# Moving the making of the up projection's first operands, pinning the down projection's splits, and loading w_up's pass from another queue

## The chip, the core and the metric

The kernel runs on one core of a Trainium2 chip. The metric is the device time of one execution in microseconds. A core has TensorE (PE; its weight loads are listed as PEld), VectorE (DVE), ScalarE (ACT), GpSimd (POOL) and SyncE (SP), which here only issues DMAs. Each engine works through its own instructions in order.

## The reference

It is one decoder layer over 2048 rows of width 1024, in float32. `h2` below goes through an FFN of width 2816 with a causal convolution of three taps over the rows.

```python
h = rmsnorm(x, norm1_g) * (1 + sc1) + sh1
proj = h @ w_in                                   # q, k, v, forget logits, x_in, B, C
attn = forgetting_attention(q, k, v, logf)        # 8 heads of 64
conv = bg * causal_dwconv(cg * xin, conv_mix_w)
x = x + g1 * (concatenate([attn, conv]) @ w_out)
h2 = rmsnorm(x, norm2_g) * (1 + sc2) + sh2
u = causal_dwconv(h2 @ w_up, ffn_conv_w)
u_gate, u_val = split(u, 2)
return x + g2 * ((silu(u_gate) * u_val) @ w_down)
```

## The kernel before

To keep float32 accuracy, every matrix product is made from operands that are split in two: a rounded part `hi` and the rest `lo = raw - hi`. `mm3` (line 138) then issues three matmuls, hi·hi, hi·lo and lo·hi. A split costs one ACT operation for `hi` (L720) and one DVE operation for `lo` (L721).

The stages follow each other in the program:

- **Projections and short convolution** (to about 635 us). `project` makes k and then q in blocks of 128 rows. Beside them, `magnitudes` (lines 585 to 596) goes over the whole of w_up once, 88 tiles of 256 KB, and sums absolute values on ACT (L590), for a scale. It has one buffer `wx`: a load (L595, on SP) is issued after the sum before it.
- **Attention** (about 635 to 966 us). Steps s = 0 to 63, eight for each head. POOL writes the tile `wide`, a transposing DMA on SP (L892) turns it into `far`. `load_out` (line 728) loads one of 16 tiles of w_out on SP, and the function that it returns multiplies it with the gate g1 on POOL (L733).
- **Output projection** `mixed(Q)` for four quarters of 512 rows, in two halves of columns, each over eight k: 16 steps n. A step splits a tile of w_out and a tile of the mixed input. `side` is another generator, of which one part is run at the steps listed in `at`.
- **`norm2(Q)`** makes the operands of the up projection for a quarter: `columns` transposes on PE (L1047) and applies scale and shift on ACT (L1049), `operand` makes a float16 pair (ACT L1037, DVE L1038). The product h2 @ w_up is made for two quarters at once with seven block products in place of eight (a Strassen-like scheme), so the operands are sums and differences named b11, b21, b22, t1 to t4. For Q = 1, b22 and t4 are left to `norm2_rest` (lines 1101 to 1105), which calls `columns` once more.
- **`up(hv)`** for the halves hv = 0, 1 of the rows: 22 iterations, one for each 128 columns of the gate and the value. An iteration has seven products of 12 matmuls (L1167). `up_weights(i)` (line 1122) is a generator that loads two tiles of w_up, scales them (ACT L1132), and makes their sums and float16 pairs (DVE L1107, L1108, L1114; ACT L1111). It runs one iteration ahead. `finish(i)` (taps L1180, silu, product L1192, store to `y_sc`) runs one iteration behind.
- **`down(Q, hf)`**, four calls after each `up`: 22 pairs of tiles of y and w_down, loaded together into one raw tile (L1262, L1263), split, and multiplied.

The order in which a queue gets its instructions is made by a scheduler from the program's order and a model of the durations. `K(...)` pins an instruction: pinned instructions of an engine keep the program's order among themselves. All of `up` is pinned. The splits of `mixed` and `down` are not.

Tiles with one tag share a fixed number of buffers: `raw` 4, `hi` and `lo` 4 each, `t2` (`temp()`) 7.

Of the kernel before, what the change touches and what calls it, by code (L numbers as in the profile page):

```python
# [1 line left out]

# [6 lines left out]
F32 = mybir.dt.float32  # L9
# [35 lines left out]
def kernel(  # L45
# [102 lines left out]
    with ExitStack() as ph:  # L148
# [437 lines left out]
        def magnitudes():  # L586

            while up_tiles:
                n, t = up_tiles.pop(0)
                K(A.activation(t, t, AF.Abs, accum_out=l1[:, n : n + 1]))  # L590
                seen[0] = n + 1
            for n in range(seen[0], min(seen[0] + 1, 88)):
                t = bp.tile([P, 512], F32, tag="wx", name="wx", bufs=1)
                k, i = divmod(n, 11)
                K(nc.sync.dma_start(t, w_up[k * P : (k + 1) * P, i * 512 : (i + 1) * 512]))  # L595
                up_tiles.append((n, t))

        def up_scales():
# [151 lines left out]
    def mixed(Q, side=iter(()), at=()):  # L750

        rows = [slice((Q * 4 + t) * P, (Q * 4 + t + 1) * P) for t in range(4)]
        n = 0
        if Q:
            places(Q)
        if Q == 0:
            kept[0] = [raw_tile() for _ in range(4)]
        elif Q == 1:
            kept[1] = [wide_temp()[:, 0:D] for _ in range(4)]
        for hf in range(2):  # L760
            n0 = hf * 512
            acc = [ps_d.tile([P, 512], F32, tag="d", name="acc") for _ in range(4)]
            ops = []
            for k in order:
                if hf == 0 and (Q or k == 3):
                    load_mixed(Q, k)
                (mh, ml), (wh, wl) = halves(pair_tiles())
                split(wo[k, hf], wh, wl)
                split(src[Q, k], mh, ml)
                ops.append((mh, ml, wh, wl))  # L770
                for t in () if k == 2 else range(4):
                    for o in ops:
                        a, b = [m[:, t * P : (t + 1) * P] for m in o[:2]]
# [4 lines left out]
                if n in at:  # L778
                    next(side, None)
                if Q < 2 and n == (2, 4)[Q]:  # L780
                    for xp, r in zip(kept[Q], rows):
                        K(nc.sync.dma_start(xp, x[r, :]))
                if Q >= 2 and k == 0:
                    kept[Q] = [temp() for _ in range(4)]
                    for xp, r in zip(kept[Q], rows):
                        K(nc.sync.dma_start(xp, x[r, n0 : n0 + 512]))
                yield
            for t in range(4):
                xp = kept[Q][t]
                if Q < 2:  # L790
                    xp = xp[:, n0 : n0 + 512]
                V.tensor_tensor(xp, acc[t], xp, op=ALU.add)
                if Q >= 2:
                    G.dma_start(x1_sc[Q * 4 + t][:, n0 : n0 + 512], xp)
                elif hf:
                    G.dma_start(x1_sc[Q * 4 + t], kept[Q][t])


    with ExitStack() as ph:
# [159 lines left out]
        for s in range(H * nu + 8):  # L959
            h, u = divmod(s, nu)  # L960
            run = []
            if h < H:
                if u == 0:
                    steps = []
                    if h + 1 < H:
                        heads[h + 1], steps = load_head(h + 1)
                    if h % 2 == 0:
                        if h:
                            v16.append(load_values(h // 2))
                        at = cp.tile([P, NT, P], F32, tag="at", name="at")  # L970
                elif h + 1 < H:
                    steps[u - 1]()
                units.append({"h": h, "u": u, "at": at})
            for back, stage in ((1, weights), (0, scores), (2, turn), (4, values)):
                if 0 <= s - back < H * nu:
                    run.append(stage(units[s - back]))
            if s >= 16 and s % 16 in (0, 4):
                slow.append(store(units[s - 5]["at"], (s - 16) // 16, (0, 3) if s % 16 == 0 else (1, 2)))
            if s >= (H - 4) * nu and s % 2 == 0 and s < H * nu:
                gated = load_out((s - (H - 4) * nu) // 2)  # L980
            if s == (H - 1) * nu:
                places(0)
# [12 lines left out]
            if (H - 4) * nu <= s < H * nu and s % 2:  # L995
                gated()
            if s == H * nu:
                first = mixed(0)
            if s >= H * nu:
                next(first)  # L1000
# [11 lines left out]
    with ExitStack() as ph:  # L1012
# [47 lines left out]
        def norm2(Q):  # L1060
# [18 lines left out]
            for k in range(4):  # L1079
# [5 lines left out]
                b1 = columns(Q, k)  # L1085
                yield
                b2, t3 = columns(Q, 4 + k), temp()
                if Q == 3:
                    operand("b22", k, b2)
                diff(t3, b2, b1)  # L1090
                for e in bt["b11", k]:
                    diff(b1, b1, e)
# [1 line left out]
                diff(b2, b2, b1)  # L1094
                operand("t2", k, b2)
                operand("t3", k, t3)
                if Q == 3:
                    last_operands(Q, k)
                yield

        def norm2_rest(Q):
            for k in range(4):
                operand("b22", k, columns(Q, 4 + k))
                last_operands(Q, k)
                yield

# [10 lines left out]

        def up_pair():
            used[0] += 1
            return [fb.tile([P, 1024], F16, tag=f"wo{used[0] % 8}{e}", name="pair") for e in range(2)]  # L1120

        def up_weights(i):

            raws = raw_tile(), raw_tile()
            for raw, ct in zip(raws, (i, NPAIR + i)):
                nc.sync.dma_start(
                    raw.rearrange("p (k n) -> p k n", n=P), w_up[:, ct * P : (ct + 1) * P].rearrange("(k p) n -> p k n", p=P)
# [25 lines left out]
            low(raws[1], *pc)  # L1153
            yield

        def up(hv, side):


            def product(acc, pair, name, first):
# [33 lines left out]
                nc.sync.dma_start(y_sc[i][:, hv * 1024 : (hv + 1) * 1024], yv)  # L1193
                yield

            wts = up_weights(0)
            ops = next(wts)
            for _ in range(5):
                next(wts)
            last = None  # L1200
            for i in range(NPAIR):
                o11, o12, os2, os4, os3, o22, os1 = ops
# [9 lines left out]
                next(side, None)  # L1212
# [3 lines left out]
                K(A.activation(p1, X, AF.Copy))  # L1216
# [6 lines left out]
                next(side, None)  # L1223
# [6 lines left out]
                next(side, None)  # L1230
# [4 lines left out]
                next(side, None)  # L1235
                p5 = temp()
                K(A.activation(p5, Z, AF.Copy))
                product(Y, os3, "t3", False)
# [11 lines left out]
            for _ in last:  # L1250
                pass

        def down(Q, hf):
            n0 = hf * 512
            acc = [ps_d.tile([P, 512], F32, tag="d", name="acc") for _ in range(4)]
            w = [None] * NPAIR
            order = [(i, t) for i in range(NPAIR - 2) for t in range(4)]
            order += [(i, t) for t in range(4) for i in range(NPAIR - 2, NPAIR)]
            for i, t in order:
                if w[i] is None:  # L1260
                    raw = raw_tile()
                    nc.sync.dma_start(raw[:, 0:512], y_sc[i][:, Q * 512 : (Q + 1) * 512])  # L1262
                    nc.sync.dma_start(raw[:, 512:1024], w_down[i * P : (i + 1) * P, n0 : n0 + 512])  # L1263
# [12 lines left out]
            pass  # L1276
        for _ in mixed(1, norm2(0), (1, *range(5, 13))):
            pass
        steps = norm2(1)
        for _ in mixed(2, steps, (1, 5, 7, 10, 11, 14, 15)):  # L1280
            pass
        for _ in mixed(3, steps, (2, 3)):
            pass
        for hv in range(2):
            up(hv, iter(()) if hv else norm2_rest(1))
            for n in range(4):
                down(2 * hv + n // 2, n % 2)
                if hv == 0 and n < 2:
                    for _ in norm2(2 + n):
                        pass  # L1290
# [28 lines left out]
```

## Time and profile before

| what | value |
|---|---|
| three runs, median | 2508.15 us (2499.21 to 2508.64) |
| the profiled execution | 2507.0 us |
| its span, first to last instruction of the program | 2505.3 us |
| mean granted clock of TensorE | 0.989 |
| `up(0)`, first to last product | 1169.3 to 1596.2 us |
| four calls of `down` | 1596.2 to 1848.7 us |
| `up(1)` | 1848.5 to 2259.0 us |
| four calls of `down` | 2259.1 to 2500.8 us |

In a line of instructions the columns are line, engine, operation, names of what is written and read, shapes and count; then busy time and mean duration in ns; then the idle time of the engine ahead of them and who ended it. A line of waits has who waited, for whom, the sum in us, how often, and the longest. A line of windows has the window, its length, and for each engine the busy time and the count of instructions, then the granted clock of TensorE, the mean busy share of the DMA engines, and GB/s.

### The profile page before, as it was taken

The page shows a single profiled execution, that of the slowest core. Times are in us where ns is not written, and L with a number is a line of the kernel's source. Part 1 is how long each engine was busy: PE and PEld are TensorE (multiplying, and loading weights), DVE is VectorE, ACT ScalarE, POOL GpSimd, SP SyncE. Part 2 cuts the span into 40 slices and gives each one's busy share as a digit, 9 for nine tenths or more (in the row PEclk, how much of TensorE's full clock was granted, in tenths as well). Part 3 has the DMA queues.
Part 4 walks back from the last instruction along what each step waited for, and adds up shares of the span by engine and source line. Part 5 has one row for each costly group of instructions (what it writes and reads, how often), then busy time and mean ns, then how long its engine had stood idle before and what let it go on. Part 6 is the DMA issues. An engine that isn't in the chain of part 4 may idle for free. (4 is left out here: it accounts for less than half of the span.)

```text
span 2505.3 us, 38577 instructions
## 1 busy us (share of the span) xinstructions
PE 2388.9 (95%) x14432; PEld 1655.5 (66%) x14432; DVE 1814.0 (72%) x3377; ACT 1292.5 (52%) x2068; POOL 375.4 (15%) x314
## 2 busy tenths in 40 slices
PE   4999999999899889998999999999999999999999
PEld 4988778888677667776444444678764444447887
DVE  7567784342899887676888988667859888885554
ACT  3533443210788776554656566355545555553333
POOL 4210001011577873110000000000000000000000
PEclk9999999999999999999999999999999999999999
DMA  8444786433789997143222222567742222235775
GB/s 237 148 123 127 196 238 182 147 112 89 149 173 184 189 183 196 72 140 123 67 85 85 92 85 93 191 214 235 219 142 92 84 93 84 85 122 168 230 228 186
DMA packets 429348, 368.71 MB, mean 147 GB/s; under 512 B 184336, under 2 KB 328040, under 8 KB 428136
## 3 DMA queue, kind: packets, MB, share of 16 engines
q1 hardware_dynamic: 421976, 349.40, 50.0%
q10 hardware_dynamic: 4752, 8.46, 0.9%
q0 software_dynamic: 2432, 8.39, 0.9%
q8 instruction: 113, 1.85, 0.3%
q14 instruction: 75, 0.61, 0.1%
HBM read 267.54 MB, written 65.08 MB: 133 GB/s over the span
## 5 line engine op out<-in xcount | busy, mean ns | idle before, releaser
L1167 PEld LDWEIGHTS <-pair 128*128 128x128 f16 x3696 | 364.5, 99 | 470.2 <-issue 36.4
L1167 PE MATMUL acc<-t,pair 128*128 128x512 f16 x2112 | 482.5, 382 | 6.5 <-DVE t L1107 6.5
L1167 PE MATMUL acc<-b,pair 128*128 128x512 f16 x1584 | 372.5, 386 | 17.2 <-DVE pair L1114 6.6
L141 PE MATMUL acc<-hi 128*128 128x512 f32 x960 | 378.5, 395 | 7.9 <-ACT hi L720 5.7
L141 PE MATMUL acc<-hi,lo 128*128 128x512 f32 x960 | 375.8, 391 | 0.2 <-DVE lo L721 0.2
L141 PE MATMUL acc<-lo,hi 128*128 128x512 f32 x960 | 375.1, 391 | 0.0
L721 DVE TENSOR_TENSOR lo<-raw,hi 128x1024 fp32r<-128x1024 f32 (+1 forms) x208 | 236.3, 1142 | 178.8 <-ACT hi L720 178.6
L720 ACT ACTIVATE hi<-raw 128x1024 fp32r<-128x1024 f32 (+1 forms) x208 | 204.9, 991 | 240.4 <-PE acc L141 207.7
L1180 DVE SCALAR_TENSOR_TENSOR w<-w,fcw,w 128x1024 f32<-128x1024 f32 x176 | 226.1, 1285 | 39.9 <-ACT w L1175 30.8
L141 PEld LDWEIGHTS acc<-hi 128*128 128x128 f32 x960 | 180.7, 188 | 48.2 <-ACT hi L720 6.8
L141 PEld LDWEIGHTS acc<-hi,lo 128*128 128x128 f32 x960 | 180.6, 188 | 39.7 <-DVE lo L721 1.5
L141 PEld LDWEIGHTS acc<-lo,hi 128*128 128x128 f32 x960 | 180.6, 188 | 37.0 <-DVE lo L721 0.8
L1111 ACT ACTIVATE pair<-raw 128x1024 f16<-128x1024 f32 x132 | 138.2, 1049 | 70.9 <-DVE raw L1108 70.9
L1175 ACT ACTIVATE w<-w,fcw 128x1024 f32<-128x1024 f32 x88 | 100.7, 1144 | 131.9 <-DVE w L1107 131.9
L879 ACT ACTIVATE s_t<-s_t,nb,cst 128x2048 f32<-128x2048 f32 (+15 forms) x128 | 164.7, 1288 | 5.7
L1114 DVE TENSOR_TENSOR pair<-raw,pair 128x1024 f16<-128x1024 f32 x132 | 160.7, 1219 | 3.9 <-ACT pair L1111 3.9
L590 ACT ACTIVATE wx<-wx 128x512 f32<-128x512 f32 x88 | 55.6, 632 | 202.1 <-DMA wx<-in_w_up_dram 192.5
L141 PE MATMUL pr<-hh,wh 128*128 128x512 f32 x384 | 153.9, 401 | 0.0
L141 PE MATMUL pr<-hh,wl 128*128 128x512 f32 x384 | 151.5, 394 | 2.1 <-DVE wl L178 2.1
L141 PE MATMUL pr<-hl,wh 128*128 128x512 f32 x384 | 151.6, 395 | 0.0
L891 POOL TENSOR_TENSOR wide<-s_t,wide 128x1024 f16<-128x1024 f32 x64 | 136.8, 2138 | 5.3
L862 DVE CUSTOM_DVE_ANT_0 s_t<-ps,nf,mx 128x512 f32<-128x512 f32 (+1 forms) x192 | 119.2, 643 | 16.3 <-PE ps L841 8.0
(278 smaller groups left out, 4568.6 us busy)
## 6 DMA issues: line engine op xcount, KB each, us to landing
raw<-in_w_up_dram SPq DMA_DIRECT2D x88, 512.0 KB, 3.7
raw<-y_sc SPq DMA_DIRECT2D x176, 256.0 KB, 4.3
raw<-in_w_down_dram SPq DMA_DIRECT2D x176, 256.0 KB, 4.3
wx<-in_w_up_dram SPq DMA_DIRECT2D x88, 256.0 KB, 2.8
y_sc<-w SPq DMA_DIRECT2D x44, 512.0 KB, 2.6
wm<-in_w_ada_dram SPq DMA_DIRECT2D x128, 128.0 KB, 2.9
wr<-in_w_in_dram SPq DMA_DIRECT2D x40, 256.0 KB, 4.2
x_t<-in_x_dram SPq DMA_DIRECT2D x16, 512.0 KB, 5.3
```

The source lines that it names most:

```text
L141: ins = T.matmul(acc, lhsT=a, rhs=b, start=st, stop=sp)
L590: K(A.activation(t, t, AF.Abs, accum_out=l1[:, n : n + 1]))
L720: A.activation(hi, raw, AF.Copy, scale=HS)
L721: V.tensor_tensor(lo, raw, hi.bitcast(F32), op=ALU.subtract)
L862: K(V.tensor_tensor_reduce(out=s_t[:, o0 + c0 : o0 + c0 + cw], in0=ps[:, 0:cw], in1=nf[:, c0 : c0 + cw], scale=1.0, scalar=-3.0e38 if g == ...
L879: K(A.activation(cols, cols, AF.Exp, bias=nb[:, p : p + 1], scale=qk[:, 4:5], accum_out=un["l"][:, p : p + 1]))
L891: K(G.tensor_tensor(wide[:, 1, :], s_t[:, WB * P : WU], wide[:, 0, :], op=ALU.subtract))
L1111: K(A.activation(hi, raw, AF.Copy))
L1114: K(V.tensor_tensor(lo, raw, hi, op=ALU.subtract))
L1167: K(T.matmul(acc, lhsT=a, rhs=b, start=st, stop=sp, skip_group_check=True))
L1175: K(A.activation(y, u[:, 0:1024], AF.Copy, scale=fcw[:, ct : ct + 1]))
L1180: K(V.scalar_tensor_tensor(y, u[:, m : m + 1024], fcw[:, m * 44 + ct : m * 44 + ct + 1], y, op0=ALU.mult, op1=ALU.add))
```

## The change

Five edits, and what follows from them:

1. `norm2_rest` is gone. `norm2(1)` makes b22 and t4 itself, from the columns that it has, as `norm2(3)` did already.
2. The first part of `up_weights(0)` (its loads and five of its steps) is now a generator `first_weights`. For hv = 0 it follows `norm2(1)` as the side work of `mixed(2)` and `mixed(3)`, whose lists of steps are new; for hv = 1 it is side work of the fourth `down`. Its two raw tiles have buffers of their own (tag `first`), and the pairs of weights take the buffers of w_out in the order in which `mixed` is done with them.
3. `down`'s splits are pinned (`split_pair`). In iteration 21 of `up`, where there are no next weights, `first_pairs` loads the first three pairs of `down` and splits them at three of the places where `up_weights` steps stood.
4. w_out's 16 tiles are loaded at every fourth step of the whole attention, and gated two steps later; before, at every second step of its second half, and gated one step later.
5. The loads of `magnitudes` are issued from ACT's queue.

```diff
-                K(nc.sync.dma_start(t, w_up[k * P : (k + 1) * P, i * 512 : (i + 1) * 512]))
+                K(nc.scalar.dma_start(t, w_up[k * P : (k + 1) * P, i * 512 : (i + 1) * 512]))
...
-            if s >= (H - 4) * nu and s % 2 == 0 and s < H * nu:
-                gated = load_out((s - (H - 4) * nu) // 2)
+            if s % 4 == 0 and s < H * nu:
+                gated = load_out(s // 4)
...
-            if (H - 4) * nu <= s < H * nu and s % 2:
+            if s % 4 == 2 and s < H * nu:
                 gated()
...
                 b2, t3 = columns(Q, 4 + k), temp()
-                if Q == 3:
-                    operand("b22", k, b2)
+                operand("b22", k, b2)
...
-                if Q == 3:
-                    last_operands(Q, k)
-                yield
-
-        def norm2_rest(Q):
-            for k in range(4):
-                operand("b22", k, columns(Q, 4 + k))
                 last_operands(Q, k)
                 yield
...
-            raws = raw_tile(), raw_tile()
+            raws = [raw_tile() if i else fp.tile([P, 1024], F32, tag="first", name="raw", bufs=2) for _ in range(2)]
...
+        def first_weights():
+
+            wts = up_weights(0)
+            ready["ops"] = next(wts)
+            ready["wts"] = wts
+            for _ in range(5):
+                next(wts)
+                yield
+
+        def first_pairs(Q):
+
+            raws = [load_pair(Q, 0, i) for i in range(3)]
+            yield
+            for i, raw in enumerate(raws):
+                ready[i] = split_pair(raw)
+                yield
+            while True:
+                yield
...
+        def split_pair(raw):
+            hi, lo = pair_tiles()
+            K(A.activation(hi, raw, AF.Copy, scale=HS))
+            K(V.tensor_tensor(lo, raw, hi.bitcast(F32), op=ALU.subtract))
+            y, wd = halves((hi, lo))
+            return (*y, *wd)
...
-            wts = up_weights(0)
-            ops = next(wts)
-            for _ in range(5):
-                next(wts)
+            wts, ops = ready.pop("wts"), ready.pop("ops")
...
-                wts = up_weights(i + 1) if i + 1 < NPAIR else iter([None] * 9)
+                wts = up_weights(i + 1) if i + 1 < NPAIR else first_pairs(2 * hv)
...
-            w = [None] * NPAIR
+            w = [ready.pop(i, None) for i in range(NPAIR)]
...
-                    y, wd = halves(split(raw, *pair_tiles()))
-                    w[i] = (*y, *wd)
+                    w[i] = split_pair(load_pair(Q, hf, i))
+                if t == 0 and i >= NPAIR - 8:
+                    next(side, None)
...
-        steps = norm2(1)
-        for _ in mixed(2, steps, (1, 5, 7, 10, 11, 14, 15)):
+        steps = chain(norm2(1), first_weights())
+        for _ in mixed(2, steps, (1, 4, 7, 10, 13, 16)):
             pass
-        for _ in mixed(3, steps, (2, 3)):
+        for _ in mixed(3, steps, (2, 5, 8, 12, 13, 14, 15, 15, 16)):
             pass
         for hv in range(2):
-            up(hv, iter(()) if hv else norm2_rest(1))
+            up(hv)
             for n in range(4):
-                down(2 * hv + n // 2, n % 2)
+                steps = first_weights() if hv == 0 and n == 3 else iter(())
+                down(2 * hv + n // 2, n % 2, steps)
+                for _ in steps:
+                    pass
```

More of the change, by code (lines that the diff above doesn't have):

```diff
@@ L1 @@
 from contextlib import ExitStack
+from itertools import chain
 import concourse.bass as bass
@@ L777, in mixed @@
                 n += 1
-                if n in at:
+                for _ in range(at.count(n)):
                     next(side, None)
@@ L1119, in up_pair @@
             used[0] += 1
-            return [fb.tile([P, 1024], F16, tag=f"wo{used[0] % 8}{e}", name="pair") for e in range(2)]
+            return [fb.tile([P, 1024], F16, tag=f"wo{order[(used[0] - 1) % 8]}{e}", name="pair") for e in range(2)]
         def up_weights(i):
-            raws = raw_tile(), raw_tile()
+            raws = [raw_tile() if i else fp.tile([P, 1024], F32, tag="first", name="raw", bufs=2) for _ in range(2)]
             for raw, ct in zip(raws, (i, NPAIR + i)):
@@ L1154, in up_weights, with load_pair, up @@
             yield
-        def up(hv, side):
+        ready = {}
+        def first_weights():
[13 more added lines that the diff above has]
+                yield
+        def load_pair(Q, hf, i):
+            raw = raw_tile()
+            nc.sync.dma_start(raw[:, 0:512], y_sc[i][:, Q * 512 : (Q + 1) * 512])
+            nc.sync.dma_start(raw[:, 512:1024], w_down[i * P : (i + 1) * P, hf * 512 : (hf + 1) * 512])
+            return raw
+        def split_pair(raw):
[4 more added lines that the diff above has]
+            return (*y, *wd)
+        def up(hv):
             def product(acc, pair, name, first):
@@ L1211, in up @@
                 product(X, o11, "b11", True)
-                next(side, None)
-                wts = up_weights(i + 1) if i + 1 < NPAIR else iter([None] * 9)
+                wts = up_weights(i + 1) if i + 1 < NPAIR else first_pairs(2 * hv)
                 ops = next(wts)
@@ L1222, in up @@
                 product(Y, os2, "t2", True)
-                next(side, None)
                 u2 = temp()
@@ L1229, in up @@
                 product(X, o12, "b21", False)
-                next(side, None)
                 K(A.activation(gate[:, 2:514], X, AF.Copy))
@@ L1234, in up @@
                 product(Z, os1, "t1", True)
-                next(side, None)
                 p5 = temp()
@@ L1251, in up, with down @@
                 pass
-        def down(Q, hf):
+        def down(Q, hf, side=iter(())):
             n0 = hf * 512
             acc = [ps_d.tile([P, 512], F32, tag="d", name="acc") for _ in range(4)]
-            w = [None] * NPAIR
+            w = [ready.pop(i, None) for i in range(NPAIR)]
             order = [(i, t) for i in range(NPAIR - 2) for t in range(4)]
```

3 lines of the change are left out of this document (removed).

## The prediction

> **What bounds the kernel now.** I read the page first, then the busy time by windows over the FFN, cut at the iterations of `up`, then the waits inside the bad iterations.
>
> ```profile
> span 2505.3 us, 38577 instructions
> ...
> PE 2388.9 (95%) x14432; PEld 1655.5 (66%) x14432; DVE 1814.0 (72%) x3377; ACT 1292.5 (52%) x2068; POOL 375.4 (15%) x314
> ```
>
> PE is busy 95% of the span, so only its 5% idle time, and time at a lowered clock, can be won. I looked for them where the change is. In the next view the columns are window, its length, busy time of the products of L1167 and their count, granted clock, DMA share, GB/s. Each window is one iteration of `up` (84 products; the 85th is an overlap): iterations 0, 1, 20, 21 of the first half (hv=0), then 0, 1, 20 of the second.
>
> ```profile
> 1169.27:1209.43 40.16, 25.31 (x84) 0.79 0.13 42
> 1209.43:1227.56 18.13, 18.13 (x85) 1.00 0.27 88
> 1553.90:1577.85 23.95, 20.77 (x85) 0.87 0.54 165
> 1577.85:1596.39 18.54, 18.54 (x85) 0.98 0.35 115
> 1848.54:1873.30 24.76, 21.17 (x84) 0.86 0.24 76
> 1873.30:1891.43 18.13, 18.13 (x85) 1.00 0.28 88
> 2217.75:2241.08 23.33, 19.98 (x85) 0.93 0.54 163
> ```
>
> An undisturbed iteration takes 18.13 us. Five of these seven take longer: +22.03, +5.82, +0.41, +6.63, +5.20, together 40.1 us. The waits of PE in the first of them, then in iteration 20 of each half (the second line of that fence is what ACT waited for there), then in iteration 0 of hv=1:
>
> ```profile
> PE acc L1167 <- ACT t L1237: 6.1, 1, 6.1
> ...
> PE acc L1167 <- ACT t L1216: 4.5, 1, 4.5
> ...
> PE acc L1167 <- DVE pair L1114: 3.0, 1, 3.0
> ```
> ```profile
> ACT hi L720 <- DMA raw<-in_w_down_dram: 3.8, 3, 2.2
> PE acc L1167 <- DVE t L1107: 3.2, 1, 3.2
> ```
> ```profile
> PE acc L1167 <- DVE pair L1114: 3.6, 1, 3.6
> ```
>
> The start of `up` waits for its first weights (L1114) and for ACT and DVE, which are making `norm2_rest`. The end of `up` is different: L720 is the split of `down`. The scheduler has put `down`'s unpinned splits ahead of `up`'s own steps on ACT and DVE, they wait for their loads, and the sums behind them come late.
>
> **The change part by part.**
>
> *1. `norm2_rest` goes into `norm2(1)`.* Its rows inside the first window:
>
> ```profile
> L1049 ACT ACTIVATE t<-pt,sh,a 128x512 f32<-128x512 f32 x4 | 3.1, 771 | 3.1 <-PE pt L1047 3.1
> L1038 DVE TENSOR_TENSOR t<-t,t 128x512 f16<-128x512 f32 x4 | 2.8, 692 | 2.8 <-ACT t L1037 2.8
> ...
> L1047 PE MATMUL pt<-ident,w 128*128 128x128 f32 x16 | 2.4, 273 | 0.0
> ```
>
> The 16 transposes (2.4 us of PE) and 4 activations (3.1 us of ACT) vanish, because `norm2(1)` has these columns already. The 20 DVE operations (5 for each k, 0.69 us) and 8 ACT conversions are moved under `mixed(2)` and `mixed(3)`.
>
> *2. `up_weights(0)` moves up.* Two loads, two scalings, three conversions on ACT; on DVE 5 operations of 0.69 and 2 of 1.22 us. For hv=0 they lie in `mixed(3)` (steps 12 to 15), for hv=1 beside pairs 14 to 19 of the fourth `down`. Their raws get two buffers of their own, so SP can issue the loads early. With 1 and 2, both starts of `up` find their operands: 22.03 and 6.63 us go. I keep 1.0 and 0.3 us for the first weights being just in time.
>
> *3. `down`'s splits are pinned, and three pairs are loaded and split inside iteration 21.* No split stands ahead of `up`'s steps any more: 5.82 + 0.41 and 5.20 us go. What is late next is `finish(21)`, which now stands ahead of the fourth split on DVE. Its present run (start, length, operations):
>
> ```profile
> 1594.01 0.69 DVE L1107 TENSOR_TENSOR w<-t,acc 128x512 f32<-128x512 f32 x1 [1.10 <-PE acc L1167]
> 1595.98 2.61 DVE L1180 SCALAR_TENSOR_TENSOR w<-w,fcw,w 128x1024 f32<-128x1024 f32 x2 [1.28 <-ACT w L1175]
> 1598.50 0.68 DVE L1107 TENSOR_TENSOR w<-t,acc 128x512 f32<-128x512 f32 x1
> 1600.40 2.61 DVE L1180 SCALAR_TENSOR_TENSOR w<-w,fcw,w 128x1024 f32<-128x1024 f32 x2 [1.22 <-ACT w L1175]
> 1602.93 1.22 DVE L721 TENSOR_TENSOR lo<-raw,hi 128x1024 fp32r<-128x1024 f32 x1
> 1604.06 1.22 DVE L1192 TENSOR_TENSOR w<-w,w 128x1024 f32<-128x1024 f32 x1
> ```
> ```profile
> 1596.20:1656.50 60.30, 60.30 (x267) 49.66 (x266) 33.36 (x30) 23.73 (x24) 0.00 (x0) 1.00 0.69 221
> ```
>
> The second fence is the first `down`: 267 matmuls in 60.30 us, 0.226 us each. Three ready pairs are 36 matmuls, 8.1 us; with one more that needs only `hi`, PE can run to 1596.2 + 8.4 = 1604.6. The product of L1192 could start at 1603.0 and end at 1604.2, the fourth `lo` at 1605.4. So 0.8 us of stall is left at each end (0 if DVE runs a little earlier, 3 if a load is late). `down` itself stays as it is: ACT (23.73) and DVE (33.36) have half of its 60.30 us free, which is also the cover for the weights of hv=1.
>
> Sum of 1 to 3: 40.1 − 1.3 − 1.6 = 37.2 us gained.
>
> *4. What the cover costs.* The two halves of `mixed(3)`, DVE alone:
>
> ```profile
> 1121.80:1147.50 25.70, 18.75 (x30) 1.00 0.49 155
> 1147.50:1169.30 21.80, 10.35 (x16) 1.00 0.47 152
> ```
>
> DVE does 29.1 us there in 47.5. By the new step places `mixed(3)` makes the second parts of k=2 and k=3 (12 DVE operations each, where it made one of 7): 17 more at 0.69 is 11.7 us; the weights add 5.9. That is 46.7 us of 47.5, with the splits that PE waits for in the same queue. Back to back such operations overlap by some 0.1 us (1602.93 + 1.22 against 1604.06 above), so it fits, but narrowly. The added temp in `last_operands` also holds one of seven buffers on which SP's pinned x loads, and the loads of m_at behind them, wait. The present stalls of this kind:
>
> ```profile
> PE acc L141 <- ACT hi L720: 3.8, 2, 2.0
> ```
> ```profile
> 1083.16:1091.16 8.00, 5.94 (x22) 4.33 (x21) 3.19 (x5) 3.80 (x7) 0.00 (x0) 0.79 0.00 0
> ```
>
> Bounds: −4 us (both stalls go) to +10 (three new ones of 2.0 us with their clock loss). I take +3: one new stall of 2.0 us with the 0.79 of the clock over 8 us that goes with it (1.7 us more), less a little. The Trainium skill (TensorE: Matmul & The Clock Gate, "Why this matters for your kernels") asks only that PE not idle for more than about 3 us at a time; by that a 2 us stall keeps the clock, and this term would be +2. The row above speaks against it here: 2.0 us of idle, then 0.79.
>
> *5. w_out's loads and gates spread over the whole attention* (every fourth step, not every second one of the last half). Two equal stretches of attention, and who made PE wait in the second half:
>
> ```profile
> 640.00:775.00 135.00, 124.33 (x1859) 95.50 (x1858) 125.91 (x406) 116.28 (x223) 96.47 (x60) 1.00 0.92 182
> 775.00:910.00 135.00, 119.25 (x1807) 93.02 (x1805) 115.18 (x372) 107.01 (x204) 103.77 (x68) 0.99 0.95 184
> ```
> ```profile
> PE po L935 <- DMA far<-wide: 6.5, 3, 3.9
> ```
>
> The second stretch, with the loads and gates, does 52 matmuls less and has 6.5 us of waits for the transposing DMA. Half of the loads on SP, and of the gates on POOL, move to the first half. Bounds −6.5 to +6.5; I take −3, since the crowding is halved where it hurt.
>
> *6. w_up's pass on ScalarE's queue.* ACT in the k projection (168 to 252 us), the transposes of that stretch (four for each block of 128 rows), and the issues:
>
> ```profile
> L590 ACT ACTIVATE wx<-wx 128x512 f32<-128x512 f32 x23 | 14.5, 632 | 53.5 <-DMA wx<-in_w_up_dram 51.8 <-DVE rqy L123 1.8
> ```
> ```profile
> 168.00:252.00 84.00, 8.22 (x56) 1.00 0.51 133
> ```
> ```profile
> wx<-in_w_up_dram SPq DMA_DIRECT2D x88, 256.0 KB, 2.8
> ...
> v_sc<-vt ACTq DMA_DIRECT2D x16, 256.0 KB, 2.2
> ...
> m_cv<-y ACTq DMA_DIRECT2D x16, 256.0 KB, 4.3
> ```
>
> With one buffer a load starts when the sum before it is done, and ACT waits it out: 23 in 84 us, 3.65 us each. The issue itself moves into that wait (51.8 us for 23), so it costs nothing there. Behind a waiting sum stand the squares and conversions that PE's accumulators and weights need. If the load takes as long from ACT's queue as from SP's, the price is 0, which I take (it is the same transfer). From ACT's queue 256 KB took 2.2 and 4.3 us, so the bounds are −0.6 and +1.5 us for each load. Faster loads can win at most PE's waits for weights at the change to the q projection, 4.0 us and about as much again in clock:
>
> ```profile
> PE acc L141 <- ACT wh L177: 2.3, 2, 1.5
> PE acc L141 <- DVE wl L178: 1.7, 2, 1.1
> ```
>
> Sum of all: −37.2 + 3 − 3 + 0 = −37.2 us. The profiled execution took 2507.0 us, 1.2 under the median of the three runs, so both give 2470.
>
> **The rivals.**
>
> *A, DVE becomes the bound of `mixed(3)`.* For it: 46.7 of 47.5 us. Against: DVE can run three splits ahead, and spill-over finds iteration 0 of `up`, which has no `finish` yet. If the 17.6 added us push the splits, some 15 come back: 2485.
>
> *B, the pins do not hold the ends of `up`.* If the three early loads land late, the pinned splits stop ACT inside iteration 21 as the unpinned ones did in 20, and the 9.8 us of part 3 stay: 2480. Against: two raw buffers are free from early in iteration 20.
>
> *C, slower: the queue of ACT.* PE needs 84/14 = 6.0 us for a block, and ACT's 23 loads per 14 blocks also make 1.64 × 3.65 = 6.0 us. So from the first tenth by which a load takes longer on ACT's queue, PE follows ACT. With +1.5 us over the some 45 loads of both projections it is 67 us: 2507 − 37 + 67 = 2537. Over 0.8 us each it eats the whole gain.
>
> *D, the side effects are all good* (attention −6.5, stalls of `mixed` gone, projections some better): 2457.
>
> **How the numbers follow.** Forecast 0.66, A 0.12, B 0.08, C 0.09 (half of it near no change), D 0.05. Runs of this kernel can tell about 0.5%, 12.5 us. The forecast, A, B and D are all faster by more: 0.91; same 0.04, slower 0.05. Range 2450 to 2490: from D with some of part 6's gain, to A with a worse attention; it leaves out C and the far ends.
>
> **What would show it.** Right: iterations 0 and 20 of both halves at 18 to 19 us, no L1047 in the first, L721 only in iteration 21 and later, PE under 1 us idle at the fourth pair of each first `down`. Part 4: `mixed(3)` over 50 us shows A. Part 6: a mean above 3.7 us between sums of L590 in the k projection shows C. I am wrong if iteration 0 of hv=0 still waits for L1114, or if the time won in `up` turns up again ahead of 1169 us.

## The result and the profile after

The changed kernel takes 2572.9 us (median of four runs, 2572.6 to 2573.2) against 2508.4 before (four runs): ratio 1.0266, 95% interval 1.0242 to 1.0290. It is slower, where 2470 us and "faster" were forecast. The profiled execution, page of the changed kernel:

```profile
span 2571.4 us, 38436 instructions
...
PE 2403.5 (93%) x14416; PEld 1664.7 (65%) x14416; DVE 1820.0 (71%) x3377; ACT 1295.9 (50%) x2064; POOL 374.6 (15%) x314
```

PE's share fell from 95 to 93%. Each row of the next table is the time from the first product of a stage to the first product of the next (in the last row, to the last product of all), taken from the traces. After is the changed kernel; e1, e5 and e14 are experiments told below.

| stage, us | before | after | e1 | e5 | e14 |
|---|---|---|---|---|---|
| projections, from the span's start | 634.4 | 645.7 | 647.6 | 631.8 | 631.3 |
| attention | 331.9 | 340.0 | 337.8 | 336.4 | 332.7 |
| mixed(0), mixed(1) | 103.3 | 104.7 | 102.9 | 104.6 | 103.2 |
| mixed(2), mixed(3) | 99.7 | 112.3 | 112.8 | 112.5 | 104.7 |
| up(0) | 426.9 | 398.7 | 398.7 | 398.7 | 400.7 |
| four downs | 252.3 | 319.4 | 251.4 | 252.8 | 254.2 |
| up(1) | 410.5 | 398.7 | 398.7 | 398.7 | 398.7 |
| four downs | 241.8 | 247.2 | 240.0 | 240.3 | 240.5 |

`up` won 40.0 us. Everything else lost: 11.3, 8.1, 1.4, 12.6, 67.1 and 5.4 us, together 105.9, and the first four downs are nearly two thirds of that. The iterations of `up` that the prediction showed, now (windows of the changed kernel, same columns):

```profile
1202.73:1220.87 18.14, 18.14 (x85) 8.21 (x85) 10.62 (x14) 6.08 (x11) 0.91 (x2) 1.00 0.23 75
1565.30:1583.43 18.13, 18.13 (x85) 8.23 (x84) 16.14 (x19) 10.84 (x17) 0.00 (x0) 1.00 0.28 88
1583.43:1601.42 17.99, 17.99 (x86) 8.12 (x84) 13.94 (x15) 8.75 (x14) 0.00 (x0) 1.00 0.64 195
1920.81:1938.95 18.14, 18.14 (x86) 8.24 (x86) 11.53 (x16) 6.10 (x10) 0.00 (x0) 1.00 0.13 50
2283.40:2301.50 18.10, 18.10 (x85) 8.23 (x84) 16.10 (x19) 10.62 (x15) 0.00 (x0) 1.00 0.28 88
```

Iterations 0, 20, 21, 0 and 20 all run undisturbed. The downs of the first half, in the kernel before and then in the changed kernel (there the second and fourth window lie between two downs):

```profile
1656.50:1722.10 65.60, 64.47 (x298) 52.21 (x297) 41.42 (x56) 37.23 (x47) 0.00 (x0) 1.00 0.73 234
1722.10:1786.90 64.80, 64.40 (x298) 52.00 (x297) 60.74 (x91) 43.90 (x59) 0.00 (x0) 1.00 0.66 201
```
```profile
1662.00:1687.50 25.50, 9.75 (x34) 5.75 (x33) 11.80 (x29) 15.50 (x24) 0.00 (x0) 0.57 0.17 59
1687.50:1750.30 62.80, 62.76 (x264) 51.37 (x264) 30.65 (x28) 23.03 (x23) 0.00 (x0) 0.96 0.73 221
1750.30:1795.00 44.70, 9.68 (x32) 5.74 (x32) 37.21 (x68) 22.04 (x36) 0.00 (x0) 0.55 0.07 24
1795.00:1857.00 62.00, 61.94 (x264) 50.70 (x265) 30.47 (x28) 24.50 (x24) 0.00 (x0) 0.97 0.65 201
```

Before, a down took its 264 matmuls and the 32 transposes of `norm2` together (298 by the overlaps). Now the transposes lie in stretches of 25.5 and 44.7 us of their own, in which PE does nothing else, and its granted clock is 0.57 and 0.55. ACT's order at the end of the second stretch shows why (L1038 is `norm2`'s float16 conversion, L1178 the `hi` of a pinned split of `down`):

```profile
1789.22 1.36 ACT L1038 ACTIVATE t<-t 128x512 f16<-128x512 f32 x2 [2.13 <-DVE t L1041]
1793.39 0.63 ACT L1038 ACTIVATE t<-t 128x512 f16<-128x512 f32 x1 [2.81 <-DVE t L1058]
1793.93 3.88 ACT L1178 ACTIVATE hi<-raw 128x1024 fp32r<-128x1024 f32 x4
```

Four splits stand ready and start only after the last operation of `norm2(3)`. The same on DVE at a later change of down (L1030 is the last gated sum of the down before):

```profile
1858.26 0.69 DVE L1030 TENSOR_TENSOR t<-t,t 128x512 f32<-128x512 f32 x1 [0.36 <-DMA t<-x_sc]
1858.87 4.63 DVE L1179 TENSOR_TENSOR lo<-raw,hi 128x1024 fp32r<-128x1024 f32 x4
```
```profile
1860.14 0.63 PE L142 MATMUL acc<-lo,hi 128*128 128x512 f32 x1 [1.69 <-DVE lo L1179]
```

The gated sum needs the end of a down's matmuls, so the next down's first `lo` can't be early: PE stands idle for 1.6 to 1.7 us at each of the four such changes. That gave theory P: a pinned instruction stands behind whatever the program gave its engine just before, pinned or not.

### The profile page after: what moved, and what is told of

Read it like the earlier page. It is cut to its first block, busy times and chain, and to the rows that moved or that the text cites. A ratio compares the mean times of both kernels' runs of the same rounds, so it can differ in the third digit from the quotient of the medians.

```text
span 2571.4 us, 38436 instructions
## 1 busy us (share of the span) xinstructions
PE 2403.5 (93%) x14416; PEld 1664.7 (65%) x14416; DVE 1820.0 (71%) x3377; ACT 1295.9 (50%) x2064; POOL 374.6 (15%) x314
## 4 chain that ended last, share of the span: by engine, by line
PE 71%; DMA 11%; DVE 9%; ACT 4%; POOL 3%; issue 3%; SPq 0%; ACTq 0%; POOLq 0%; DVEq 0%
PE acc L1194 31%; PE acc L142 22%; PE pr L142 10%; DMA wx<-in_w_up_dram 4%; DMA far<-wide 4%; PE pv L142 2%; POOL wide L892 1%; DVE acc L235 1%; DVE t L1041 1%; PE pt L900 1%; PE ps L839 1%; POOL wide L891 1%; PE ps L840 1%; DMA vt<-v_sc 1%; DVE near L907 1%
## 5 line engine op out<-in xcount | busy, mean ns | idle before, releaser
L1194 PE MATMUL acc<-b,pair 128*128 128x512 f16 x1584 | 363.4, 379 | 0.0
L1179 DVE TENSOR_TENSOR lo<-raw,hi 128x1024 fp32r<-128x1024 f32 x176 | 213.3, 1224 | 194.2 <-ACT hi L1178 193.9
L1178 ACT ACTIVATE hi<-raw 128x1024 fp32r<-128x1024 f32 x176 | 184.7, 1058 | 265.3 <-PE acc L142 225.0
```

The lines of the kernel that those rows point to most:

```text
L1178: K(A.activation(hi, raw, AF.Copy, scale=HS))
L1179: K(V.tensor_tensor(lo, raw, hi.bitcast(F32), op=ALU.subtract))
L1194: K(T.matmul(acc, lhsT=a, rhs=b, start=st, stop=sp, skip_group_check=True))
```

## The experiments

All ratios are to the kernel before, timed on the same chip.

| kernel | median us | ratio, 95% interval |
|---|---|---|
| e1 later splits free | 2496.1 | 0.9963 (0.9950 to 0.9976) |
| e2 w_up's pass on SP | 2556.6 | 1.0203 (1.0183 to 1.0223) |
| e3 w_out's loads late | 2558.5 | 1.0212 (1.0193 to 1.0231) |
| e4 before, with pins alone | 2584.8 | 1.0318 (1.0299 to 1.0338) |
| e5 three edits back | 2478.6 | 0.9885 (0.9863 to 0.9907) |
| e6 a second DMA issue | 2568.6 | 1.0245 (1.0226 to 1.0264) |
| e7 other steps | 2489.3 | 0.9926 (0.9907 to 0.9944) |
| e8 eight temps | 2481.6 | 0.9899 (0.9872 to 0.9927) |
| e9 norm2 inside down | 2559.8 | 1.0213 (1.0195 to 1.0230) |
| e10 finer parts | 2480.5 | 0.9897 (0.9882 to 0.9912) |
| e11 weights back | 2479.7 | 0.9895 (0.9880 to 0.9909) |
| e12 rest back | 2477.3 | 0.9886 (0.9871 to 0.9900) |
| e13 rest behind copies | 2475.7 | 0.9893 (0.9866 to 0.9920) |
| e14 rest split | 2473.2 | 0.9883 (0.9852 to 0.9913) |
| e15 e5, loads spread | 2482.5 | 0.9920 (0.9895 to 0.9945) |
| e16 e5, ACT's queue | 2490.4 | 0.9947 (0.9931 to 0.9964) |

### The pins: e1, e4, e9

e1 takes them from the changed kernel, but for the three early pairs:

```diff
-                    w[i] = split_pair(load_pair(Q, hf, i))
+                    w[i] = split_pair(load_pair(Q, hf, i), lambda op: op)   # not K
```

> The changed kernel with the pins taken from down's splits, except those of the three pairs in iteration 21 of up. Theory P (a pinned split stands behind whatever its engine was given just before it in the program, so the first splits of downs 1 and 2 wait for the last ACT and DVE work of norm2, and those of every later down for the last gated sum of the down before): the two stretches of 25.4 and 44.8 us between downs 0, 1 and 2 vanish, and the 1.7 us at each other change of down too; the four downs of the first half go from 319.4 us back to about 252, the time from 2573 to 2500-2508. Rival W (the work of norm2 and of the moved weights itself is too much for ACT and DVE beside down): order alone changes little, 2555-2575.

e4 adds them to the kernel before:

```diff
-                    y, wd = halves(split(raw, *pair_tiles()))
+                    hi, lo = pair_tiles()
+                    K(A.activation(hi, raw, AF.Copy, scale=HS))
+                    K(V.tensor_tensor(lo, raw, hi.bitcast(F32), op=ALU.subtract))
+                    y, wd = halves((hi, lo))
```

> The kernel before with one edit: all of down's splits pinned where the program has them, with no pairs made early. Theory P: norm2 runs alone between downs 0, 1 and 2 as in the changed kernel, +67 us, +5 at the other changes of down; the ends of up lose their 11 us of stall, and the first split of each first down now stands behind finish(21), 5 to 9 us each: 2575-2590. Rival W: the pins cost nothing by themselves, 2495-2515.

Both came out as theory P had it: 77 us less in e1 (2572.9 − 2496.1, by ratios 76; it is 4 us below the lower end of what was expected), and 0.0318 × 2506.6 = 80 us more in e4. Downs 1 and 2 of e1, then e4's two stretches between downs:

```profile
1660.20:1725.20 65.00, 64.51 (x298) 52.23 (x297) 41.41 (x56) 37.26 (x47) 0.00 (x0) 1.00 0.74 235
1725.20:1789.90 64.70, 64.30 (x298) 51.96 (x297) 60.65 (x92) 43.86 (x59) 0.00 (x0) 1.00 0.64 201
```
```profile
1660.00:1685.30 25.30, 9.68 (x32) 5.74 (x32) 11.63 (x28) 15.45 (x24) 0.00 (x0) 0.58 0.15 54
...
1748.20:1793.00 44.80, 9.74 (x34) 5.80 (x33) 37.31 (x69) 22.11 (x36) 0.00 (x0) 0.55 0.06 24
```

DVE and ACT do the same work in e1 as in the kernel before, 60.65 of 64.70 us in down 2, and it fits beside the matmuls. So not the work costs but the order. e4 also shows the pins' good side: its iterations 20 and 21 take 18.13 us each in both halves, and then the first split, behind `finish(21)`, stops PE at the start of each first down:

```profile
1595.98 1.65 PE L141 MATMUL acc<-hi 128*128 128x512 f32 x3 [5.84 <-ACT hi L1265]
```

That stall the early pairs remove. e9 keeps all pins of the changed kernel and moves the neighbours:

```diff
-                if t == 0 and i >= NPAIR - 8:
+                if t == 0 and i in at:
...
+                if hv == 0 and n:
+                    steps, at = (norm2(1 + n), range(4, 22, 2)) if n < 3 else (first_weights(), range(14, 22))
-                if hv == 0 and n < 2:
-                    for _ in norm2(2 + n):
-                        pass
```

> The changed kernel, all its pins kept, with norm2(2) and norm2(3) run as side work of downs 1 and 2, one part at every second pair from pair 4 on, not between the downs. Theory P (a pinned split stands behind what its engine was given just before it): the stretches of 25.4 and 44.8 us without products of down vanish though every split is pinned, the four downs go from 319.4 to 252-262 us, the time from 2573 to 2503-2516; the 1.7 us at each change of down stays. Rival: pinned splits are slow in themselves (no run-ahead), 2540-2575.

The number that theory P was given here fell: only 13 us were won, and the time lies in the range of the rival, by which pinned splits are slow in themselves. Downs 1 and 2 of e9, the waits of PE in down 2, and ACT's order at one of them:

```profile
1660.26:1729.10 68.84, 66.92 (x298) 51.50 (x296) 38.71 (x53) 37.27 (x47) 0.00 (x0) 1.00 0.59 187
1729.10:1841.70 112.60, 79.09 (x298) 59.61 (x297) 68.59 (x98) 44.52 (x58) 0.00 (x0) 0.82 0.42 135
```
```profile
PE acc L142 <- ACT hi L1178: 28.3, 4, 7.1
```
```profile
1769.05 0.63 ACT L1038 ACTIVATE t<-t 128x512 f16<-128x512 f32 x1 [2.81 <-DVE t L1058]
1769.59 1.99 ACT L1178 ACTIVATE hi<-raw 128x1024 fp32r<-128x1024 f32 x2
```

The short parts of `norm2(2)` do lie between the splits now: the stretch and down 1 took 25.5 + 62.8 = 88.3 us and take 68.8. But each second part of `norm2(3)` ends with a conversion on ACT behind eleven of the part's twelve operations on DVE, and the next pinned `hi` stands behind that conversion: four stalls of 7.1 us inside down 2 in place of one stretch ahead of it. They are 28.3 of the 48 us by which down 2 is longer than in the kernel before; another 14.7 us are longer busy time of PE (79.09 against 64.40 us) at a granted clock of 0.82. The rival is answered by the first down of the changed kernel, whose splits are all pinned and which has no `norm2` ahead of it:

```profile
1602.00:1662.00 60.00, 60.00 (x263) 48.85 (x262) 32.95 (x31) 23.17 (x24) 0.00 (x0) 1.00 0.71 230
```

It runs as fast as in the kernel before (60.30 us for 267 matmuls), so pinned splits aren't slow in themselves. The mechanism holds; what I had missed is that a pinned split waits for its neighbour wherever the neighbour stands.

### The two sets of loads: e2, e3, e5, e15, e16, e6

```diff
-                K(nc.scalar.dma_start(t, w_up[k * P : (k + 1) * P, i * 512 : (i + 1) * 512]))   # e2
+                K(nc.sync.dma_start(t, w_up[k * P : (k + 1) * P, i * 512 : (i + 1) * 512]))
```

e3 puts back the three lines of part 4 of the change, e5 makes the edits of e1, e2 and e3 at once, e15 those of e1 and e2, e16 those of e1 and e3.

> The changed kernel with the loads of w_up's pass back on SP's queue. Theory Q (from ACT's queue a load lands in 3.3 us, not 2.8, and PE follows the pass in both projections): landing median back to 2.8 us, the first product of attention back from 645.7 to about 635, the time from 2573 to 2560-2564. Rival N (the shift of the projections has another cause): the first product of attention stays at 644-647 and the time at 2570-2576.

> The changed kernel with w_out's 16 tiles loaded and gated in the second half of attention only, as before the change. Theory L (the spread costs attention its 8 to 9 us, since the transposing loads of the first half now queue behind w_out's loads on SP): attention, first product to first product of the output projection, goes from 340 back to about 332 us, the time from 2573 to 2563-2567. Rival K (attention is longer because it is entered in another phase, after slower projections): it stays at 338-342 and the time at 2570-2576.

> The changed kernel with three edits at once: only the three early pairs pinned in down, w_up's pass on SP's queue, w_out's loads in the second half of attention. If the three prices add up (76.8, 16.3 and 14.4 us), 2573 - 107.5 = 2465, within 2460-2471. Rival: they overlap (a later start hides part of another's stall), 2475-2490.

> The kernel of the three edits back, but w_out's loads spread over the whole attention as in the changed kernel (w_up's pass on SP). Theory L (the spread has a price of its own): 8 to 14 us more than the three edits back. Theory K (the spread costs only behind a pass on ACT's queue, or attention's length varies by some us with its phase): within 4 us.

> The kernel of the three edits back, but w_up's pass loaded from ACT's queue (w_out's loads in the second half). Theory Q (the queue has a price of its own): 10 to 17 us more than the three edits back. If instead the two prices hide each other: 3 to 8 us.

One at a time, the queue gave back 16 us (e2) and the loads 14 us (e3), by medians and by ratios, each some 4 us more than the most that was expected. Together on top of e1 they gave 17.5 (2496.1 − 2478.6; by ratios 20), so e5 missed its 2460 to 2471 and fell into the range of its rival: the prices do not add up. By ratios and 2508 us the queue costs 0.0062 × 2508 = 16 us with the loads late (e16 − e5) and 11 with them spread (e1 − e15); the spread costs 9 us on SP's queue (e15 − e5) and 4 on ACT's (e1 − e16), both with intervals that overlap. Theory Q holds: the first product of attention comes at 642.9 to 647.6 us in five kernels with w_up's pass on ACT's queue (after, e1, e3, e9, e16), and at 630.2 to 634.4 in twelve with it on SP's (before, e2, e4, e5, e7, e8, e10 to e15). But PE does not follow the pass all the way, as theory Q had it. Up to attention PE runs the same 3040 instructions in the same order in the kernel before and in the changed kernel, so they can be compared one by one. Between 60 and 240 us of the kernel before they come no later in the changed one; they come 2.5 us later at 271 us, 5.9 at 332, 11.8 at 344, and 11.4 from 378 us to the start of attention, though loads of the pass still run. So nearly the whole loss is made in the q projection (264 to 356 us) and at its two ends. For the spread, attention took 337.4 to 342.4 us in five kernels that have it (after, e1, e2, e9, e15), and 330.4 to 337.7 in twelve that don't (before, e3, e4, e5, e7, e8, e10 to e14, e16): means 339.8 and 334.4. Theory L has the sign, with some 5 us; theory K has the scatter, 7 us between kernels with the same loads (by its median alone, 3.9 us over e5, e15 would have been K's).

e6 was to tell whether ACT's queue costs by its issue or by its landing. It is e5 with a tiny second DMA beside each load:

```diff
+                K(nc.scalar.dma_start(none[n : n + 1, :], w_up[n : n + 1, 0:64]))
                 K(nc.sync.dma_start(t, w_up[k * P : (k + 1) * P, i * 512 : (i + 1) * 512]))
```

> The kernel of the three edits back (w_up's pass loaded by SP), and beside each of its 88 loads a second one of 256 bytes from DRAM to DRAM, issued by ACT at the same place. Theory I (what costs is the issue of 0.33 us in ACT's own order, behind the sum): 8 to 14 us more than the three edits back. Rival D (what costs is that the 256 KB land 0.5 us later from ACT's queue): within 3 us of the three edits back.

It took 90 us more than e5, which neither theory had. The landing of the same loads, in the changed kernel and then in e6, and ACT's sums in the stretch from 168 to 252 us in both:

```profile
wx<-in_w_up_dram ACTq DMA_DIRECT2D x88, 256.0 KB, 3.3
```
```profile
wx<-in_w_up_dram SPq DMA_DIRECT2D x88, 256.0 KB, 4.2
...
none<-in_w_up_dram ACTq DMA_DIRECT2D x88, 0.2 KB, 2.5
```
```profile
L591 ACT ACTIVATE wx<-wx 128x512 f32<-128x512 f32 x23 | 14.6, 633 | 48.6 <-DMA wx<-in_w_up_dram 48.6
```
```profile
L591 ACT ACTIVATE wx<-wx 128x512 f32<-128x512 f32 x17 | 10.7, 631 | 63.3 <-DMA wx<-in_w_up_dram 63.3
```

With 256 bytes more on another queue, 256 KB land 1.4 us later than the 2.8 us of before, a sum comes every 84/17 = 4.9 us, and PE comes late with it: mixed(0) starts 89 us later than in e5. So the mechanism of rival C is real. In the changed kernel the delay was small: still 23 sums in 84 us. As the second DMA itself slowed the loads, e6 doesn't tell issue from landing; that stays open.

### The 13 us of mixed: e7, e8, e10 to e14

All start from e5; e10 has the eight temps of e8 too. The list of steps in e7, then e8's temps, then e10's cut:

```diff
-        for _ in mixed(2, steps, (1, 4, 7, 10, 13, 16)):
+        for _ in mixed(2, steps, (1, 3, 4, 7, 10, 11)):
-        for _ in mixed(3, steps, (2, 5, 8, 12, 13, 14, 15, 15, 16)):
+        for _ in mixed(3, steps, (2, 6, 9, 11, 12, 13, 14, 15, 16)):
```
```diff
-NTEMP = 7
+NTEMP = 8
```
```diff
                 operand("t1", k, b1)
+                if Q == 1:
+                    yield    # three such, and steps range(1, 17), range(2, 17)
```

> The kernel of the three edits back, with other steps for the work under mixed(2) and mixed(3): (1, 3, 4, 7, 10, 11) and (2, 6, 9, 11 to 16), so that the second parts of norm2(1), with their four temps, stand ahead of the steps at which x is loaded into four of the seven temps. Theory T (mixed is 13 us longer since x's pinned loads on SP wait for temps, and the loads of m_at behind them): 4 to 9 us less than the three edits back. Rival A (the added DVE work itself): within 3 us of them, or slower.

> The kernel of the three edits back with eight temps in place of seven (paid for by one of the two buffers of the first weights, which takes a free wide temp). Theory T: SP's waits for temps in mixed(2) and mixed(3) go, 4 to 9 us less than the three edits back. Rival A (the added DVE work itself): within 3 us.

> The kernel of the three edits back with eight temps, and the second part of norm2(1) for each k cut into four parts, one part run at each step of mixed(2) and mixed(3) from the first on. Theory B (blocks of up to 12 operations on DVE hold up the splits that PE needs next): mixed(2) and mixed(3) together go from 112.7 us to 102-107, 5 to 10 us less in all. Rival A (the amount of added work costs, however cut): within 3 us of the three edits back.

Theory T fell: with an eighth temp PE's waits in mixed(2) and mixed(3) are those of e5 (6.3 us for `hi`, 4.4 us for `lo`), and e7 was 11 us slower than e5. Theory B fell too: cut finer, mixed(2) and mixed(3) took 112.8 us. What is left is rival A, the amount of added work, tested by moving it out. It is not the amount alone: in e7 the same work at other steps made the two stages 118.8 us long. e11 makes the weights at the start of `up(0)` again. e12 puts `norm2_rest` back with its four parts in iteration 0, e13 the same with each part behind a pinned copy or sum, and e14 splits them:

```diff
+                if Q == 3 or k == 3:                      # e14; k = 0 by islice(rest, 1) in mixed(3)
+                    last_operands(Q, k)
...
                 K(A.activation(p1, X, AF.Copy))
+                next(side, None)                          # e13, e14: behind the copy
```

> The kernel of the three edits back, with the first weights of the first half made at the start of up again. If the weights are what lengthens mixed(3): mixed(2) and mixed(3) go from 112.7 us to about 106, iteration 0 of up gets 6 to 9 us, the sum within 3 us of the three edits back. If it is norm2's added work (b22 and t4): mixed stays at 110-113 and the time is 6 to 9 us longer.

> The kernel of the three edits back, with b22 and t4 of norm2(1) made in iteration 0 of up again (16 transposes more), mixed's old steps, and the first weights still under mixed(3). If norm2's 20 DVE operations are what lengthens mixed: mixed(2) and mixed(3) go from 112.7 us to 100-104, iteration 0 of up stays under 21 us, 5 to 11 us less in all. If it is the weights: mixed stays at 108-113, and the time is the same or up to 4 us longer.

> The kernel of e12 (b22 and t4 made in iteration 0 of up), each of the four parts now behind a pinned copy of a product's sum on ACT (p1, the sum u2, the gate, p5) and not ahead of it. Theory O (order: the two stalls of 3.1 and 2.6 us came from copies that stood behind a part): iteration 0 goes from 29.3 us to 20-24, 5 to 9 us less than e12. Theory A (amount of DVE work): 27 us or more, within 3 us of e12.

> As e13, but b22 and t4 of k = 3 are made directly in norm2(1), those of k = 0 in mixed(3), and only k = 1 and 2 in iteration 0, behind p1 and the gate's copy. Theory A: DVE has room for about 10 of the 20 operations in each place; mixed(2) and mixed(3) stay under 102 us, iteration 0 under 21, 8 to 12 us less than e12. Theory O: about as e13.

| us | before | e5 | e11 | e12 | e13 | e14 |
|---|---|---|---|---|---|---|
| mixed(2), mixed(3) | 99.7 | 112.5 | 108.4 | 98.1 | 99.7 | 104.7 |
| iteration 0 of up(0) | 40.2 | 18.1 | 22.5 | 29.3 | 30.0 | 20.1 |
| sum | 139.9 | 130.7 | 130.8 | 127.4 | 129.7 | 124.8 |

The weights cost 4 us in either place (e11 against e5), so long as b22 and t4 are under mixed; without these they cost nothing there (98.1 us in e12 with the weights, 99.7 before without them). For b22 and t4, the best of each place, 98.1 + 18.1 = 116.2 us, stands for a sum without them: they cost 14.5 us in mixed (e5), 11.2 and 13.5 in iteration 0 (e12, e13; theory O fell, e13's iteration 0 is no shorter), and 8.6 when both places take half (e14). What moves is 20 DVE operations and 8 ACT conversions together; no run tells the two apart. The numbers expected of e12 (iteration 0 under 21 us, 5 to 11 us less) and of e14 (mixed under 102 us, 8 to 12 us less than e12) were missed: by ratio e12 is level with e5, and e14 within 1 us of e12. In e14, by halves of mixed(3) and then iteration 0:

```profile
1119.30:1150.10 30.80, 25.29 (x110) 20.01 (x109) 23.86 (x39) 15.87 (x28) 2.43 (x6) 0.94 0.28 94
1150.10:1171.83 21.73, 21.73 (x98) 17.80 (x96) 16.25 (x25) 13.60 (x20) 2.13 (x5) 1.00 0.73 226
1171.83:1191.94 20.11, 19.33 (x93) 9.16 (x93) 16.41 (x23) 9.36 (x16) 0.90 (x2) 1.00 0.18 57
```

e14 is the fastest of all medians and beats both kernels (29.5 us under its runs of before, ratio 0.9883); by their intervals it can't be told from e5, e7, e8, e10 to e13 and e15.

## Why the prediction was wrong, point by point

**Starts and ends of `up` (steps 1 to 3): right.** 37.2 us were forecast, 40.0 came; the kept 2.9 us were not needed. Rival B is out. But the last sign that the prediction named for being wrong came too: the time won in `up` turned up again ahead of it, where steps 4 to 6 lost 33.4 us.

**"`down` itself stays as it is": the step that failed.** It took the pins to order the pinned instructions among themselves, and looked for free time on ACT and DVE, which there was. It never asked what the program gives these engines just ahead of each split: `norm2(2)`, `norm2(3)` and the gated sums, which the free splits used to overtake. Forecast 0, measured +67.1 and +5.4 us; e1 and e4 show it from both sides. With this term left out, the sum of the others is 33.4 lost to 40.0 won. No rival held this case, so the 0.91 for "faster" was far too sure; e1, without it, is faster by 0.37%, which is less than the 0.5% that the prediction took as the least that runs can tell, though its interval leaves out "no change".

**The cover in mixed (step 4): mechanism right, size wrong.** +3 forecast, +12.6 measured, over the upper bound of 10. Stalls of PE with a lowered clock behind them were forecast, and they came, but more of them: PE's idle time in mixed(2) and mixed(3) grew from 5.3 to 12.7 us, and its busy time from 94.4 to 99.6 us, at a granted clock of 0.94 in place of 0.98. Two halves of mixed(3), changed kernel:

```profile
1145.72:1177.90 32.18, 27.46 (x107) 21.69 (x108) 22.03 (x36) 13.66 (x24) 3.28 (x7) 0.84 0.35 113
1177.90:1202.70 24.80, 22.85 (x99) 17.84 (x97) 22.41 (x35) 16.63 (x25) 1.85 (x5) 1.00 0.52 171
```

DVE is busy 22.03 + 22.41 = 44.4 us there, close to the forecast 46.7, but the stage grew to 57, over the 50 us that were named as the sign of rival A: it did not fit, though DVE stands still a fifth of the time. So it is rival A's place and nearly its price (15), but not a DVE that is busy all the time. The temps, which step 4 also named, are not the cause (e8); which of the moved operations hold up the splits, and by their number or by their places, stays open.

**w_out's loads (step 5): wrong sign.** −3 forecast, +8.1 here, some +5 over all kernels. That spreading the loads halves the crowding was argued from the second half alone. The first half had no waits of PE for the transposing DMA; now it has (the next line: changed kernel, 645 to 815 us), and in the second half they went only from 6.5 to 5.8 us. The rest of the 8.1 us these waits don't show.

```profile
PE po L936 <- DMA far<-wide: 3.3, 3, 2.6
```

**ACT's queue (step 6): price not 0.** +11.3 us in the projections, 11 to 16 in the time. The load lands in 3.3 us, not 2.8, inside the bound of +1.5 us, so what rival C feared is there at a third of its size. The sign that I had named for it, over 3.7 us between sums in the k projection, did not show (84/23 = 3.65): the loss came behind that stretch, around the q projection. Whether the later landing makes it, or the issue on ACT, stays open (e6). The Trainium skill (DMA: Bandwidth & Descriptors, "Issuing engines are not separate DMA queues") says that starting DMAs from several engines saves only the time that the issue takes on the sequencer; the runs agree that nothing is won, and show a cost beside it, 11 to 16 us, that the Trainium skill doesn't give there.

**The last sum.** From the median of the three runs, 2508.15 − 37.2 is 2471 us and not 2470; nothing hangs on it.

## What to carry to other kernels

Before pinning an instruction, list what the program gives its engine just ahead of it, at every place where the pinned line runs, and what that waits for; free time on the engine says nothing about it. Pin only where the profile shows a wait that the pin removes (here three pairs of 22). And busy time that fits a stage on average still costs when the stage's own splits share the queue: try half of what is to be moved under it before moving all (in e14 the two stages took 124.8 us, in e5 130.7, though the whole times can't be told apart).

## What the runs showed of the hardware that was not expected

With a DMA of 256 bytes from DRAM to DRAM on ACT's queue beside each 256 KB load on SP's, such a load landed in 4.2 us (e6, row above); without it, in 2.7 us (e5). And the clock after a short stall isn't settled by the stall's length. In the changed kernel 1.69 us of idle ahead of 1860.14 was followed by 0.79, in e12 1.99 us by 1.00 (the stall's row of e12, then the windows, of the changed kernel and of e12):

```profile
1088.62 0.50 PE L142 MATMUL acc<-hi 128*128 128x512 f32 x1 [1.99 <-ACT hi L721]
```
```profile
1860.00:1868.00 8.00, 7.86 (x28) 6.35 (x29) 4.72 (x5) 2.04 (x2) 0.00 (x0) 0.79 0.83 267
```
```profile
1088.62:1096.62 8.00, 7.92 (x35) 6.24 (x36) 5.89 (x11) 3.57 (x7) 0.59 (x1) 1.00 0.07 27
```

The stall that the prediction had read shows it best. It stands at the same place, 1.99 us long, in five kernels: over the 8 us behind it the clock was 0.79 in the kernel before (1085.75 to 1093.75 us), e13 and e14, and 1.00 in e4 and e12. So the prediction's 1.7 us of clock loss for such a stall was one case of two.
